# High and low weight parts word by word in one tile, in the feature-major projections of a two-layer decoder trunk

## The chip, the cores and the metric

The kernel runs on one core of a Trainium2 chip. The metric is the device time of one execution in microseconds (us); three timed executions of the kernel before the change gave 2126.0, 2127.0 and 2125.79 us, median 2126.0. The engines in the profile are PE (TensorE, matmuls), PEld (TensorE's weight loads, which overlap PE), DVE (VectorE), ACT (ScalarE), POOL (GpSimd) and SP (SyncE, which here issues the DMAs).

## The reference

A decoder trunk of two layers over 256 positions of width 2048, in fp32. Layer A is a gated mixer beside a cross-attention into 256 memory tokens, layer B a latent attention beside the same cross-attention; each ends in an output projection and a gated feed-forward block of width 5632. Nearly all of the time is in its products with weight matrices:

```python
D_MODEL = 2048; SEQ = 256; DEPTH = 2; D_FF = 5632
...
for l in range(DEPTH):
    if l == N_A:
        kv = rmsnorm(x, g_kv) @ w_kv_a
    ...
    h = rmsnorm(x, g_mix[l])
    z = h @ w_in_a[l]            # layer A: 2048 x 3584; layer B: w_in_b, 2048 x 1024
    ...
    mo = memory_attention(q_m, mem, g_mem[l], w_mem_kv[l])
    x = x + jnp.concatenate([main, mo], axis=-1) @ w_out[l]
    x = x + conv_ffn(rmsnorm(x, g_ffn[l]), w_ffn_up[l], conv_w[l], conv_b[l], w_ffn_down[l])
return rmsnorm(x, g_final)
```

## The kernel before

**Two parts for each operand.** To come near fp32 with the faster matmul type fp32r, each activation and each weight is split in a high part (the value rounded to fp32r) and a low part (what the rounding left). `chunk` makes the two parts of a piece of a weight matrix: a DMA of 512 KB brings 128 x 1024 words into a tile `raw`, ACT writes the high part to a tile `whi` (line 117, or 122 where the rows are scaled by a gain), and DVE writes `raw` minus `whi` to a tile `wlo` (line 118 or 123). There are four tiles of each of the three kinds, used in turn. Each of the tiles holds its 1024 words one behind the other.

**Feature-major projections.** `gemm_fm` computes a product with the features on the partitions: the weights are the stationary operand (128 x 128 words for each matmul), the activations the moving one. A moving tile has 512 columns: 256 of the high part and 256 of the low part. For each 128 x 128 block of weights there are two matmuls: the high weights with all 512 columns (line 140), and the low weights with the 256 high columns (line 144). A call has mostly 16 blocks of 128 rows and 4 blocks of 128 columns, so 64 pairs of matmuls into four PSUM banks; the weights come in 8 chunks, each good for 8 pairs. `mm_fm` takes two chunks at a time (four blocks each in rows and columns) and writes the matmuls out in alternating order: high then low for one couple of chunks, low then high for the next, so that the same kind runs across the seam. When a call is through, its four banks are read out (`evict`): `join` adds the two halves of a bank (ACT line 222, DVE line 224), and in the feed-forward block a multiplication on POOL (line 571), the convolution (ACT line 574, DVE lines 575 and 576) and the gate follow.

**Token-major projections.** `gemm_tm` has the roles swapped: the activations are stationary and the weights move, 512 columns at a time (lines 182 to 184). It serves the memory values, one half of layer A's input projection, layer B's values and the last layer's down projection.

**Order.** The order of each engine's instructions is fixed at build time by a scheduler that replays the program against its own model of the chip; each engine takes its instructions in that order. Tiles come from pools: a tile that is used again waits until all readers of its former content are through. All weight DMAs are issued from SP's queue, each when a `raw` tile is free.

The other callers of `chunk` keep the tiles' layout as it was: `gemm_tm`, the small rotary key projection (`twice`) and layer B's queries (`heads`).

Of the kernel before, what the change touches and what calls it, by code (L numbers as in the profile page):

```python
# [8 lines left out]
F32 = mybir.dt.float32  # L9
F32R = mybir.dt.float32r  # L10
I32 = mybir.dt.int32
BF16 = mybir.dt.bfloat16
AF = mybir.ActivationFunctionType
ALU = mybir.AluOpType
AX = mybir.AxisListType

P = 128
# [13 lines left out]
THETA = 10000.0  # L31
EPS = 1e-6
FF_GROUPS = (4, 4, 3)


def exact_pieces(value, bits, count):
# [33 lines left out]
class Kernel:  # L70
    def __init__(self, ctx, tc, t, out):
        self.tc, self.nc, self.t, self.out = tc, tc.nc, t, out
        self.ctx = ctx
        self.n = 0
        pool = lambda name, bufs=1, **k: ctx.enter_context(tc.tile_pool(name=name, bufs=bufs, **k))
        self.cp = pool("cp")
        self.wp = pool("wp")
        self.ap = pool("ap")
        self.ps = pool("ps", 8, space=bass.MemoryType.PSUM)
# [9 lines left out]
        return pool.tile(shape, dt, tag=tag, name=self.uid(tag), bufs=bufs)  # L89


    def chunk(self, src, nk, ncol, gains=None, twice=False, heads=None):
        nc, n = self.nc, nk * ncol
        raw = self.wp.tile([P, 1024], F32, tag="raw", name=self.uid("raw"), bufs=4)
        hi = self.wp.tile([P, 1024], F32R, tag="whi", name=self.uid("whi"), bufs=4)
        lo = self.wp.tile([P, 1024], F32R, tag="wlo", name=self.uid("wlo"), bufs=4)
        view = lambda x: x[:, :n].rearrange("p (k c) -> p k c", k=nk)
        nc.sync.dma_start(out=view(raw), in_=src)
        if twice:
            both = lambda x: x.rearrange("p (k o c) -> p k o c", o=2, c=ncol)  # L100
            for k in range(nk):
                s = slice(k * ncol, (k + 1) * ncol)
                for o in range(2):
                    h = both(hi)[:, k, o, :]
                    nc.scalar.activation(h, raw[:, s], AF.Copy, scale=gains[k])
                    nc.vector.scalar_tensor_tensor(both(lo)[:, k, o, :], raw[:, s], gains[k], h.bitcast(F32), ALU.mult, ALU.subtract)
            return tuple(x.rearrange("p (k c) -> p k c", k=nk) for x in (hi, lo))
        if heads is not None:

            s = view(raw).rearrange("p k (h c) -> p k h c", h=2)  # L110
            for c0, c1 in ((0, heads), (heads, ncol // 2)):
                o = lambda x: view(x)[:, :, 2 * c0 : 2 * c1].rearrange("p k (h c) -> p k h c", h=2)
                nc.scalar.activation(o(hi), s[:, :, :, c0:c1], AF.Copy)
                nc.vector.tensor_tensor(o(lo), s[:, :, :, c0:c1], o(hi).bitcast(F32), ALU.subtract)
            return view(hi), view(lo)
        if gains is None:
            nc.scalar.activation(hi[:, :n], raw[:, :n], AF.Copy)  # L117
            nc.vector.tensor_tensor(lo[:, :n], raw[:, :n], hi[:, :n].bitcast(F32), ALU.subtract)  # L118
        else:
            for k in range(nk):  # L120
                s = slice(k * ncol, (k + 1) * ncol)
                nc.scalar.activation(hi[:, s], raw[:, s], AF.Copy, scale=gains[k])  # L122
                nc.vector.scalar_tensor_tensor(  # L123
                    lo[:, s], raw[:, s], gains[k], hi[:, s].bitcast(F32), ALU.mult, ALU.subtract
                )
        return view(hi), view(lo)
# [29 lines left out]
            low(jobs)  # L156

    def gemm_fm(self, src, kbs, nblk, rhs, evict, nk=2, gain=None, hooks={}):
        accs = [self.psum() for _ in range(nblk)]
        chunks = list(range(0, len(kbs), nk))  # L160
        for c0 in range(0, len(chunks), 2):
            jobs = []
            for c in chunks[c0 : c0 + 2]:
                g = None if gain is None else [gain(kbs[c + i]) for i in range(nk)]
                hi, lo = self.chunk(src(kbs[c], nk), nk, nblk * P, g)
                for b in range(nblk):
                    cols = slice(b * P, (b + 1) * P)
                    for i in range(nk):
                        kk = c + i
                        jobs.append((accs[b], hi[:, i, cols], lo[:, i, cols], rhs(kbs[kk]), kk == 0, kk == len(kbs) - 1))  # L170
            self.mm_fm(jobs, (c0 // 2) % 2)
            for c in range(c0, min(c0 + 2, len(chunks))):
                for f in hooks.get(c, ()):
                    f()
        for b in range(nblk):
            evict(b, accs[b])
# [154 lines left out]
    def gain(self, name, k):  # L331
        c = self.g[name] + k
        return self.gT[:, c : c + 1]
# [224 lines left out]
    def ffn(self, l, after=None, to_tokens=None, tokens=None):  # L558
# [5 lines left out]
        with self.tc.tile_pool(name=self.uid("ff"), bufs=1) as fp:  # L564
            g0 = 0
            for part, ng in enumerate(FF_GROUPS):
                h = self.ap.tile([P, NB, 512], F32R, tag="big", name=self.uid("h"))
# [11 lines left out]
                for g in range(g0, g0 + ng):  # L579
# [15 lines left out]
                    self.gemm_fm(self.rows(up, FF + g * 512, 512), ks, 4, lambda k: xhl[:, k, :], ev, hooks=turns)  # L595
                last = part == len(FF_GROUPS) - 1
                if last and l == 0:
# [403 lines left out]
```

## Time and profile before

| | |
|---|---|
| median of three executions | 2126.0 us |
| the profiled execution (span) | 2125.1 us |
| PE busy | 2101.5 us |
| DVE busy | 1465.7 us |
| ACT busy | 1148.7 us |
| POOL busy | 392.8 us |
| DMA | 184 GB/s over the span, 59.3% of the 16 engines' time on the weight queue |
| granted TensorE clock | 0.998 |

A row of the view by groups reads: line, engine, operation, output tile, input tiles, partitions x elements of output and inputs, count, then busy time of the group in us and mean ns of one instruction, then the idle time of the engine just before them and what ended most of it. Matmuls overlap, so that the duration of one (390 ns, say) is more than the distance to the next. A row of the timeline merges instructions of one group that follow each other: start, length from the first start to the last end, and count; the distance from one matmul to the next is (length minus the duration of one) over (count minus one).

### The profile page before, as it was taken

What the parts mean: (1) busy time and instruction counts of PE and PEld (TensorE: products, weight loads), DVE (VectorE), ACT (ScalarE), POOL (GpSimd) and SP (SyncE); (2) the same over time, 40 slices, a digit from 0 to 9 for tenths busy, and PEclk for the clock granted to TensorE, in tenths of its full rate; (3) what the DMA queues carried; (4) which work ended last, traced back from release to release, by engine and by line L of the source; (5) the groups of instructions that cost most, each with busy time, mean ns of one, the idle gap of its engine ahead of it and who ended that gap; (6) DMA issues with size and microseconds to landing.
All of it is one profiled execution on the core that took longest, in us unless ns stands there. A gap on an engine that the chain in (4) does not pass through costs nothing.

```text
span 2125.1 us, 31077 instructions
## 1 busy us (share of the span) xinstructions
PE 2101.5 (99%) x11624; PEld 1831.1 (86%) x11624; DVE 1465.7 (69%) x2186; ACT 1148.7 (54%) x1773; POOL 392.8 (18%) x378
## 2 busy tenths in 40 slices
PE   8999999999999999999999999999999999999998
PEld 7888888888888888888888788888888888888886
DVE  6655667777756777567798766677775577745775
ACT  7654654556535555356556554466553555535554
POOL 1000123312101121011254111332120121201210
PEclk9999999999999999999999999999999999999999
DMA  8565555666566665666655533665656666656664
GB/s 272 178 202 178 159 187 189 189 189 191 189 194 187 185 195 188 197 182 188 192 181 165 171 114 110 196 190 170 191 196 195 187 190 190 194 195 188 189 188 149
DMA packets 207548, 392.01 MB, mean 184 GB/s; under 512 B 14302, under 2 KB 22820, under 8 KB 207268
## 3 DMA queue, kind: packets, MB, share of 16 engines
q1 hardware_dynamic: 207252, 389.50, 59.3%
q8 instruction: 91, 1.49, 0.3%
q14 instruction: 61, 0.50, 0.1%
q10 hardware_dynamic: 144, 0.52, 0.1%
HBM read 387.88 MB, written 2.10 MB: 184 GB/s over the span
## 4 chain that ended last, share of the span: by engine, by line
PE 97%; DVE 1%; ACT 1%; DMA 1%; issue 0%; SPq 0%; DVEq 0%; ACTq 0%
PE ps L140 50%; PE ps L144 26%; PE ps L182 6%; PE ps L184 6%; PE ps L183 6%; PE ps L831 1%; DMA raw<-in_w_mem_kv 0%; PE ps L829 0%; PE ps L523 0%; PE ps L488 0%; DVE wlo L118 0%; PE ps L665 0%; PE ps L852 0%; DMA raw<-in_w_in_a 0%; PE ps L393 0%
## 5 line engine op out<-in xcount | busy, mean ns | idle before, releaser
L118 DVE TENSOR_TENSOR wlo<-raw,whi 128x1024 fp32r<-128x1024 f32 x660 | 843.1, 1288 | 490.3 <-ACT whi L117 362.4
L117 ACT ACTIVATE whi<-raw 128x1024 fp32r<-128x1024 f32 x660 | 697.2, 1058 | 702.7 <-PE ps L140 525.4
L140 PE MATMUL ps<-xhl,whi 128*128 128x512 f32 x3280 | 768.9, 390 | 0.0
L140 PEld LDWEIGHTS ps<-xhl,whi 128*128 128x128 f32 x3280 | 608.6, 188 | 121.7
L571 POOL TENSOR_TENSOR a<-js,rbc 128x256 f32<-128x256 f32 x176 | 230.5, 1323 | 1101.7 <-DVE js L224 1005.8
L144 PEld LDWEIGHTS ps<-xhl,wlo 128*128 128x128 f32 x3280 | 408.7, 192 | 9.2 <-DVE wlo L118 0.6
L144 PE MATMUL ps<-xhl,wlo 128*128 128x256 f32 x3280 | 413.4, 283 | 0.4 <-DVE wlo L118 0.4
L140 PE MATMUL ps<-h,whi 128*128 128x512 f32 x704 | 164.8, 390 | 0.0
L574 ACT ACTIVATE c<-a,cT 128x256 f32<-128x256 f32 x176 | 105.2, 598 | 96.9 <-POOL a L571 95.3
L140 PEld LDWEIGHTS ps<-h,whi 128*128 128x128 f32 x704 | 130.6, 188 | 26.0
L183 PE MATMUL ps<-wlo,h 128*128 128x512 f32 x352 | 136.8, 389 | 0.0
L182 PE MATMUL ps<-whi,h 128*128 128x512 f32 x352 | 136.6, 389 | 0.0
L184 PE MATMUL ps<-whi,h 128*128 128x512 f32 x352 | 136.3, 389 | 0.0
L140 PE MATMUL ps<-mainhl,whi 128*128 128x512 f32 x512 | 119.7, 390 | 0.0
L140 PEld LDWEIGHTS ps<-mainhl,whi 128*128 128x128 f32 x512 | 95.1, 188 | 19.1
L123 DVE SCALAR_TENSOR_TENSOR wlo<-raw,gT,whi 128x512 fp32r<-128x512 f32 x112 | 87.9, 829 | 25.2 <-ACT whi L122 23.0
L576 DVE SCALAR_TENSOR_TENSOR c<-a,cT,c 128x254 f32<-128x254 f32 x176 | 101.1, 587 | 0.0
L575 DVE SCALAR_TENSOR_TENSOR c<-a,cT,c 128x255 f32<-128x255 f32 x176 | 91.6, 539 | 11.6 <-ACT c L574 11.4
L122 ACT ACTIVATE whi<-raw,gT 128x512 fp32r<-128x512 f32 x112 | 74.7, 716 | 42.3 <-PE ps L140 20.0
L224 DVE TENSOR_TENSOR js<-ps,cr 128x256 f32<-128x256 f32 x213 | 84.1, 417 | 12.6 <-POOL a L571 12.3
L222 ACT ACTIVATE cr<-ps 128x256 f32<-128x256 f32 x243 | 79.4, 373 | 19.7 <-PE ps L140 16.5
L144 PEld LDWEIGHTS ps<-h,wlo 128*128 128x128 f32 x704 | 87.7, 191 | 2.0
(248 smaller groups left out, 1856.2 us busy)
## 6 DMA issues: line engine op xcount, KB each, us to landing
raw<-in_w_ffn_up SPq DMA_DIRECT2D x352, 512.0 KB, 4.2
raw<-in_w_ffn_down SPq DMA_DIRECT2D x176, 512.0 KB, 4.4
raw<-in_w_out SPq DMA_DIRECT2D x64, 512.0 KB, 4.1
raw<-in_w_in_a SPq DMA_DIRECT2D x56, 512.0 KB, 4.1
raw<-in_w_mem_kv SPq DMA_DIRECT2D x32, 512.0 KB, 4.8
raw<-in_w_in_b SPq DMA_DIRECT2D x16, 512.0 KB, 3.9
raw<-in_w_uq SPq DMA_DIRECT2D x12, 384.0 KB, 3.3
raw<-in_w_kv_a SPq DMA_DIRECT2D x8, 512.0 KB, 4.2
```

What stands on the lines that cost most here:

```text
L117: nc.scalar.activation(hi[:, :n], raw[:, :n], AF.Copy)
L118: nc.vector.tensor_tensor(lo[:, :n], raw[:, :n], hi[:, :n].bitcast(F32), ALU.subtract)
L123: nc.vector.scalar_tensor_tensor(lo[:, s], raw[:, s], gains[k], hi[:, s].bitcast(F32), ALU.mult, ALU.subtract)
L140: mm(acc[:, :], wh, x, start=first, stop=last)
L144: mm(acc[:, S:], wl, x[:, :S], start=False, stop=False)
L182: mm(acc, xh, wh, start=first, stop=False)
L183: mm(acc, xh, wl, start=False, stop=False)
L184: mm(acc, xl, wh, start=False, stop=last)
L571: nc.gpsimd.tensor_tensor(a, self.join(acc), rb, ALU.mult)
L574: nc.scalar.activation(c, a, AF.Identity, scale=w(2), bias=w(3))
L575: nc.vector.scalar_tensor_tensor(c[:, 1:], a[:, : S - 1], w(1), c[:, 1:], ALU.mult, ALU.add)
L576: nc.vector.scalar_tensor_tensor(c[:, 2:], a[:, : S - 2], w(0), c[:, 2:], ALU.mult, ALU.add)
```

## The change

`chunk` gets a new flag `lines`, which `gemm_fm` sets. With it the high and the low part of a chunk stand in one tile `whl` of 2048 + 64 words, word by word: high, low, high, low. ACT writes every second word, DVE reads every second word and writes the ones between, and the weight loads of the two kinds of matmul read 128 words with a step of two. The tile's content begins at `place`, a number of words from 0 to 63 that goes up by one with each call of `gemm_fm` that has four column blocks; over the kernel's 73 such calls it goes through all 64 values. The other callers get their two parts one after the other in the same kind of tile, at its start. There are four tiles `whl` in place of four `whi` and four `wlo`. A scratch area of SBUF for DMA descriptors is made smaller (4096 bytes for each partition), which gives the space for the 64 more words.

```diff
+PLACES = 64
...
+        self.place = 0
...
-        hi = self.wp.tile([P, 1024], F32R, tag="whi", name=self.uid("whi"), bufs=4)
-        lo = self.wp.tile([P, 1024], F32R, tag="wlo", name=self.uid("wlo"), bufs=4)
+        both = self.wp.tile([P, 2048 + PLACES], F32R, tag="whl", name=self.uid("whl"), bufs=4)
         view = lambda x: x[:, :n].rearrange("p (k c) -> p k c", k=nk)
         nc.sync.dma_start(out=view(raw), in_=src)
+        if lines:
+            pairs = both[:, self.place : self.place + 2 * n].rearrange("p (s t) -> p s t", t=2)
+            w, hi, lo = raw[:, :n], pairs[:, :, 0], pairs[:, :, 1]
+            if gains is None:
+                nc.scalar.activation(hi, w, AF.Copy)
+                nc.vector.tensor_tensor(lo, w, hi.bitcast(F32), ALU.subtract)
+            else:
+                for k in range(nk):
+                    s = slice(k * ncol, (k + 1) * ncol)
+                    nc.scalar.activation(hi[:, s], w[:, s], AF.Copy, scale=gains[k])
+                    nc.vector.scalar_tensor_tensor(
+                        lo[:, s], w[:, s], gains[k], hi[:, s].bitcast(F32), ALU.mult, ALU.subtract
+                    )
+            return tuple(x.rearrange("p (k s) -> p k s", k=nk) for x in (hi, lo))
+        hi, lo = both[:, :1024], both[:, 1024:2048]
...
     def gemm_fm(self, src, kbs, nblk, rhs, evict, nk=2, gain=None, hooks={}):
+        if nblk == 4:
+            self.place = (self.place + 1) % PLACES
...
-                hi, lo = self.chunk(src(kbs[c], nk), nk, nblk * P, g)
+                hi, lo = self.chunk(src(kbs[c], nk), nk, nblk * P, g, lines=True)
...
-    nc = bacc.Bacc("TRN2", target_bir_lowering=False, num_devices=1)
+    nc = bacc.Bacc("TRN2", target_bir_lowering=False, num_devices=1, dynamic_dma_scratch_size=4096)
```

The number of instructions of each kind stays the same on all engines, and PE's order changes in a handful of places by a few rows. On ACT and DVE the weight pieces and the evictions trade places. Below stands ACT at the end of one projection and in the next one of the first feed-forward block: `whi` (afterwards `whl`) is the high part of a weight chunk, `cr` and `c` belong to the eviction of a PSUM bank, `gate` and `h` are what the block makes of it. Before:

```order
L117 ACTIVATE whi_6724<-raw_6723 128x1024
L222 ACTIVATE cr_6641<-ps_6434 128x256
L222 ACTIVATE cr_6655<-ps_6435 128x256
L117 ACTIVATE whi_6762<-raw_6761 128x1024
L574 ACTIVATE c_6618<-a_6612,cT 128x256
L574 ACTIVATE c_6632<-a_6626,cT 128x256
L117 ACTIVATE whi_6768<-raw_6767 128x1024
```

and of the change:

```order
L104 ACTIVATE whl_6489<-raw_6488 128x1024
L240 ACTIVATE cr_6409<-ps_6210 128x256
L240 ACTIVATE cr_6423<-ps_6211 128x256
L592 ACTIVATE c_6386<-a_6380,cT 128x256
L592 ACTIVATE c_6400<-a_6394,cT 128x256
L104 ACTIVATE whl_6526<-raw_6525 128x1024
L247 ACTIVATE h_5990<-hv_6390 128x256
```

The high part of the sixth chunk has moved behind two steps of the eviction. DVE in the same block, where `wlo` (afterwards the output `whl`) is the low part of a chunk, `c` the convolution's second and third step, `hv` and `h` the gate's product and its split. Before:

```order
L118 TENSOR_TENSOR wlo_5548<-raw_5546,whi_5547 128x1024
L576 SCALAR_TENSOR_TENSOR c_5418<-a_5412,cT,c_5418 128x254
L589 TENSOR_TENSOR hv_5408<-gate_4993,c_5404 128x256
L118 TENSOR_TENSOR wlo_5554<-raw_5552,whi_5553 128x1024
L575 SCALAR_TENSOR_TENSOR c_5432<-a_5426,cT,c_5432 128x255
```

and of the change:

```order
L594 SCALAR_TENSOR_TENSOR c_5234<-a_5228,cT,c_5234 128x254
L607 TENSOR_TENSOR hv_5224<-gate_4825,c_5220 128x256
L607 TENSOR_TENSOR hv_5238<-gate_4825,c_5234 128x256
L105 TENSOR_TENSOR whl_5359<-raw_5358,whl_5359 128x1024
L248 TENSOR_TENSOR h_3478<-hv_5224,h_3478 128x256
L593 SCALAR_TENSOR_TENSOR c_5248<-a_5242,cT,c_5248 128x255
L105 TENSOR_TENSOR whl_5364<-raw_5363,whl_5364 128x1024
```

The low parts stand two or three rows further back among the eviction's steps.

More of the change, by code (lines that the diff above doesn't have):

```diff
@@ L89, in tmp, with chunk @@
         return pool.tile(shape, dt, tag=tag, name=self.uid(tag), bufs=bufs)
-    def chunk(self, src, nk, ncol, gains=None, twice=False, heads=None):
+    def chunk(self, src, nk, ncol, gains=None, twice=False, heads=None, lines=False):
         nc, n = self.nc, nk * ncol
         raw = self.wp.tile([P, 1024], F32, tag="raw", name=self.uid("raw"), bufs=4)
-        hi = self.wp.tile([P, 1024], F32R, tag="whi", name=self.uid("whi"), bufs=4)
-        lo = self.wp.tile([P, 1024], F32R, tag="wlo", name=self.uid("wlo"), bufs=4)
+        both = self.wp.tile([P, 2048 + PLACES], F32R, tag="whl", name=self.uid("whl"), bufs=4)
         view = lambda x: x[:, :n].rearrange("p (k c) -> p k c", k=nk)
         nc.sync.dma_start(out=view(raw), in_=src)
+        if lines:
[13 more added lines that the diff above has]
+        hi, lo = both[:, :1024], both[:, 1024:2048]
         if twice:
-            both = lambda x: x.rearrange("p (k o c) -> p k o c", o=2, c=ncol)
+            four = lambda x: x.rearrange("p (k o c) -> p k o c", o=2, c=ncol)
             for k in range(nk):
@@ L103, in chunk @@
                 for o in range(2):
-                    h = both(hi)[:, k, o, :]
+                    h = four(hi)[:, k, o, :]
                     nc.scalar.activation(h, raw[:, s], AF.Copy, scale=gains[k])
-                    nc.vector.scalar_tensor_tensor(both(lo)[:, k, o, :], raw[:, s], gains[k], h.bitcast(F32), ALU.mult, ALU.subtract)
+                    nc.vector.scalar_tensor_tensor(four(lo)[:, k, o, :], raw[:, s], gains[k], h.bitcast(F32), ALU.mult, ALU.subtract)
             return tuple(x.rearrange("p (k c) -> p k c", k=nk) for x in (hi, lo))
```

## The prediction

> **What bounds the kernel now.** I read the busy times first, then the chain of waits, then who waited for whom.
>
> ```profile
> PE 2101.5 (99%) x11624; PEld 1831.1 (86%) x11624; DVE 1465.7 (69%) x2186; ACT 1148.7 (54%) x1773; POOL 392.8 (18%) x378
> PE 97%; DVE 1%; ACT 1%; DMA 1%; issue 0%; SPq 0%; DVEq 0%; ACTq 0%
> PE ps L140 <- DVE qhl L235: 3.7, 1, 3.7
> PE ps L144 <- DVE wlo L118: 0.4, 1, 0.4
> ```
>
> TensorE is busy for 99% of the span, the chain is TensorE's for 97%, and its waits for others are a few single ones. So a gain can only come from matmuls that follow each other faster, and a loss from slower matmuls, from weight loads that no longer fit beside them, or from weight parts that come too late.
>
> How fast matmuls follow each other is read from the timeline of one couple of chunks in the feed-forward block, beside the groups by line:
>
> ```profile
> 396.27 4.00 PE L144 MATMUL ps<-xhl,wlo 128*128 128x256 f32 x32
> 400.10 7.44 PE L140 MATMUL ps<-xhl,whi 128*128 128x512 f32 x32
> L140 PE MATMUL ps<-xhl,whi 128*128 128x512 f32 x3280 | 768.9, 390 | 0.0
> L144 PE MATMUL ps<-xhl,wlo 128*128 128x256 f32 x3280 | 413.4, 283 | 0.4 <-DVE wlo L118 0.4
> L140 PEld LDWEIGHTS ps<-xhl,whi 128*128 128x128 f32 x3280 | 608.6, 188 | 121.7
> L144 PEld LDWEIGHTS ps<-xhl,wlo 128*128 128x128 f32 x3280 | 408.7, 192 | 9.2 <-DVE wlo L118 0.6
> ```
>
> Low matmuls: (4.00 - 0.283) / 31 = 0.120 us from one to the next. High ones: (7.44 - 0.390) / 31 = 0.227 us. A pair takes 0.347 us. The last column of the two load rows is what matters: beside high matmuls the loads stand idle for 121.7 us, beside low ones for 9.2 us in all. In the low runs the next load goes on nearly without a pause, so there the load has little room.
>
> How many pairs does the change touch? The groups give the counts:
>
> ```profile
> L140 PE MATMUL ps<-h,whi 128*128 128x512 f32 x704 | 164.8, 390 | 0.0
> L140 PE MATMUL ps<-mainhl,whi 128*128 128x512 f32 x512 | 119.7, 390 | 0.0
> L140 PE MATMUL ps<-memhl,whi 128*128 128x512 f32 x128 | 32.9, 410 | 3.5 <-DVE memhl L440 2.5 <-ACT whi L122 1.0
> L140 PE MATMUL ps<-chl,whi 128*128 128x512 f32 x48 | 13.5, 400 | 0.0
> ```
>
> 3280 + 704 + 512 + 128 + 48 = 4672, less the 16 of the rotary key projection, which keeps its layout: 4656 pairs in 582 chunks. One ns more or less on each pair is 4.7 us; 4656 x 0.347 us = 1616 us, three quarters of the span, is exposed to the change.
>
> **The change part by part.**
>
> *Weight loads with a step of two words.* The trace has no load with a step, so I bound it. A load alone, without a longer matmul over it, shows where plain fp32 matmuls of 128 columns follow each other, and a faster kind of load shows in the transposes:
>
> ```profile
> 1246.26 0.30 PEld L863 LDWEIGHTS ps<-pT,scratch 128*128 128x128 f32 x2
> L512 PEld LDWEIGHTS ps<-ident,mp 128*128 128x128 f32 x32 | 3.7, 140 | 0.8 <-PE ps L512 0.7
> L488 PEld LDWEIGHTS ps<-kT,qm 128*128 128x128 f32 x32 | 5.9, 190 | 0.9
> L488 PE MATMUL ps<-kT,qm 128*128 128x256 f32 x32 | 7.6, 379 | 0.0
> L937 PE MATMUL ps<-ident,xT 128*128 128x128 f32 x32 | 3.8, 272 | 0.0
> ```
>
> Two loads in 0.30 us, the last of them 0.19 us long, lie about 0.11 us apart: a load holds its path for some 110 ns, and in the low runs it has 120. Its room is about 10 ns. The transposes load just as many words (128x128 f32) in 140 ns where the others need 190, so fetching the same 512 bytes can take 50 ns less; I estimate from these rows that a plain load leaves about half of the read rate unused. With a step of two it reads a stretch twice as long at the same number of words, which would use up that rate but not exceed it. Upper bound: the load takes twice its 110 ns, the low matmuls then follow each other at some 220 ns, and the high ones stay at 227: 4656 x 0.10 = +466 us. Lower bound: the matmuls gain what fp32r costs over plain fp32, 390 against 379 ns for a matmul that streams as long, and 283 against 272 ns for the shorter one: 11 + 11 ns on each pair, 4656 x 0.022 = -102 us. I take 0, since the load needs 110 of 120 ns and the transposes' row says that the fetch has a rate in hand.
>
> The Trainium skill, in "SBUF — State Buffer", section "Specifications (TRN2)", says that SBUF is read in lines of 16 bytes and that full rate needs at least two hits on each line; a step of two words has exactly two, so by it the load stays as it is, and the sum too. No run here shows it.
>
> *The writes on ACT and DVE.* The number of words is the same, but ACT writes and DVE reads and writes with a step.
>
> ```profile
> L117 ACT ACTIVATE whi<-raw 128x1024 fp32r<-128x1024 f32 x660 | 697.2, 1058 | 702.7 <-PE ps L140 525.4 <-PE ps L184 140.4 <-ACT h L229 8.4
> L118 DVE TENSOR_TENSOR wlo<-raw,whi 128x1024 fp32r<-128x1024 f32 x94 | 120.4, 1292 | 59.6 <-ACT whi L117 41.2 <-PE ps L144 15.8 <-issue 2.6
> 370.00:630.00 260.00, 260.00 (x1494) 230.07 (x1493) 186.03 (x261) 141.02 (x198) 50.14 (x40) 1.00 0.62 189
> 1080.00:1200.00 120.00, 116.34 (x635) 101.39 (x634) 102.20 (x172) 69.18 (x139) 43.27 (x46) 0.97 0.55 174
> ```
>
> The two window rows give the busy time of PE, PEld, DVE, ACT and POOL. In the feed-forward stretch from 370 to 630 us DVE is busy for 186.0 of 260 us, 120.4 of them on the low parts (94 at 1292 ns, the second row, which is of this stretch). Nothing of their price shows until DVE is full: (260 - 186) / 120.4 = 0.61, so up to a factor of 1.6 TensorE covers it there. ACT has more room: 141 of 260. Lower bound 0. Upper bound: twice the time, 186 + 120 = 306 against 260 us, 18% on the 1616 us of pairs, +290 us. I take 0: 1292 ns for 1024 words is already slower than ACT's 1058, so the memory that takes ACT's words is not what holds DVE.
>
> *Four tiles in place of eight.* High and low part now come free together, so ACT's next high part waits for both kinds of matmul. What stands there now:
>
> ```profile
> 450.22 1.06 ACT L117 ACTIVATE whi<-raw 128x1024 fp32r<-128x1024 f32 x1 [0.74 <-PE ps L140]
> 451.83 4.00 PE L144 MATMUL ps<-xhl,wlo 128*128 128x256 f32 x32
> 453.04 2.36 DVE L118 TENSOR_TENSOR wlo<-raw,whi 128x1024 fp32r<-128x1024 f32 x2 [2.31 <-PE ps L144]
> 455.67 6.54 PE L140 MATMUL ps<-xhl,whi 128*128 128x512 f32 x28
> ```
>
> ACT wrote the high part at 450.22, as soon as the high matmuls of the old one were through. Now it waits for that chunk's low matmuls, the first eight of the run from 451.83: until 451.83 + 8 x 0.12 = 452.8. DVE can then begin at 453.9 in place of 453.04, 0.9 us later. The chunk's first use is after the other couple's 16 high matmuls, at 455.67 + 16 x 0.227 = 459.3, and its low part is needed later still. So 0.9 us disappears in more than 4 us of room. Behind ACT's wait stand the evictions in its queue, and the `raw` tile is free 0.9 us later, hence the next DMA; both have the same room. It can show where DVE is tight: from 1080 to 1200 us (last row of the windows above) it is busy for 102 of 120 us. There and in the eleven other calls of the two mixers and output projections I allow up to 0.9 us a call, bounds 0 and some 15 x 0.9 = 13 us, and take 4, a third, since most of these calls look like the stretch above.
>
> *The order on ACT and DVE, and the scratch area.* The weight pieces stand two or three rows further back among the evictions. Two convolution steps are about 1.1 us; that lies within the same room. All DMAs of weights are SP's, and their order is the same: 0.
>
> *Sum.* 2125.1 (the profiled execution) + 0 + 0 + 4 = 2129, and with the 0.9 us by which the median lies above this execution, **2130 us**.
>
> **The rivals.**
>
> *The load no longer fits (slower).* Place: the low runs. It decides from the point where a load takes over about 117 ns, 7% more than now. What speaks for it: the loads' idle time there is 9.2 us, no reserve at all. Against it: the transposes' 140 ns. Price: at a quarter more, 138 ns, the low matmuls follow each other at about 140 and not 120 ns, 4656 x 0.02 = +93 us, 2219 us. If the load took a share of the moving operand's reading, and twice as much as now, each of the two matmuls of a pair would pay its 11 ns a second time: +102 us, 2228 us. At twice the load, 2592 us.
>
> *DVE becomes the bound (slower).* From a factor of 1.6 on. Halfway between that and twice the time, at 1.8, DVE would need 186 + 96 = 282 of 260 us, 8.6% of 1616 us: +139 us, 2265 us. For it: DVE has two operands with the step, and 72% is its share already. Against it: nothing in the trace shows that a step of 8 bytes costs anything.
>
> The Trainium skill, in "Vector Engine (DVE) Microarchitecture Reference", section "5.2 Measured stream behaviour on trn2 (trn3 not measured)", speaks against the change: a port keeps its rate only over runs of two or more adjacent words, and an output that hops at each word took 1.71 ns for a column against 1.054. As an estimate from that page, L118 would be 1.6 times as long, just where DVE is full; a step of two words is not among its cases, and no run here shows it.
>
> *The matmuls get faster.* If fp32r's extra 11 ns come from weight words and moving words that meet in the same part of the memory, then another step and another place change it: for half of the places this would be -51 us, 2079 us; for all of them -102 us, 2028 us. For it: both kinds of matmul pay the same 11 ns although one is half as long, as if it came with the weights and not with the columns. Against it: the means of 390 ns are the same for moving tiles that lie in different places (the rows of `xhl`, `h` and `mainhl`).
>
> *It does nothing.* The four tiles cost nothing either: 2126 us. This is the forecast without its last term.
>
> **How the numbers follow.** I give the forecast, with 2124 to 2140 as its own range, 0.43; the load 0.23 (of this 0.07 for over 2300); DVE 0.12; the faster matmuls 0.15; other things, an order on ACT and DVE that happens to be better or worse, 0.07. What can be told from no change is 0.2%, 4.3 us. Of the forecast's 0.43, 0.23 lies within that and 0.17 above, 0.03 below. Faster: 0.15 + 0.03 + 0.02 = 0.20. Same: 0.23 + 0.01 = 0.24. Slower: 0.17 + 0.23 + 0.12 + 0.04 = 0.56. Range: 2095 leaves out two thirds of the faster case (0.10), 2300 the heavy end of the load and of DVE (0.07 + 0.03).
>
> **What would show it.** The profile of the changed kernel: the distance of low matmuls within a run (120 ns: the load fits; 140 or 220: it doesn't) and of high ones (227 ns; 216: the faster case; 238: a shared read); the loads' mean of 192 and 188 ns, and their idle time in low runs; the mean of the high part on ACT (1058 ns) and of the low part on DVE (1288 ns); DVE's idle time before the low part, which should now be ACT's doing alone; and TensorE's waits, which should stay below 20 us in all. If the distances differ from projection to projection, the place matters. The forecast is wrong if TensorE's distance in the runs moves by more than 1 ns, or if its waits for DVE grow by tens of us.

## The result and the profile after

The changed kernel takes 2154.9 us (median of four executions, 2154.5 to 2156.1): 1.0132 times the kernel before, with a 95% interval of 1.0118 to 1.0147. The profiled execution has a span of 2154.4 us, 29.3 us more than the 2125.1 before, at a granted clock of 0.996.

The busy times of the changed kernel:

```profile
PE 2127.1 (99%) x11624; PEld 1869.5 (87%) x11624; DVE 1470.4 (68%) x2186; ACT 1190.4 (55%) x1773; POOL 367.9 (17%) x378
```

The counts of instructions in this row are those of the kernel before. PE's busy time grew from 2101.5 to 2127.1 us, by 25.6; its idle time, span less busy, from 23.6 to 27.3 us, by 3.7. So nearly nine tenths of the loss lie in matmuls that follow each other more slowly, and the rest in waits. The groups that answer to those before (L156 was L140, L160 was L144; L104 and L105 write the two parts):

```profile
L156 PE MATMUL ps<-xhl,whl 128*128 128x512 f32 x3280 | 785.1, 395 | 0.0
L160 PE MATMUL ps<-xhl,whl 128*128 128x256 f32 x3280 | 415.3, 284 | 3.3 <-DVE whl L110 2.8
L156 PEld LDWEIGHTS ps<-xhl,whl 128*128 128x128 f32 x3280 | 632.8, 196 | 113.0
L160 PEld LDWEIGHTS ps<-xhl,whl 128*128 128x128 f32 x3280 | 411.9, 197 | 11.9 <-DVE whl L110 3.0
L104 ACT ACTIVATE whl<-raw 128x1024 fp32r<-128x1024 f32 x542 | 613.0, 1148 | 552.0 <-PE ps L160 258.9
L105 DVE TENSOR_TENSOR whl<-raw,whl 128x1024 fp32r<-128x1024 f32 x542 | 688.7, 1284 | 418.0 <-ACT whl L104 416.9
```

The busy time of a group of overlapping matmuls is a count times their distance, so its growth tells the distance's. The high matmuls on `xhl` have 785.1 - 768.9 = 16.2 us more, 4.9 ns each; the low ones 1.9 us, 0.6 ns each. These 18.1 us over 3280 pairs make 25.7 us over all 4656, which is PE's whole growth. The timeline shows it without a mean, in the projection that stands near the one quoted before:

```profile
402.07 4.04 PE L160 MATMUL ps<-xhl,whl 128*128 128x256 f32 x32
405.95 7.56 PE L156 MATMUL ps<-xhl,whl 128*128 128x512 f32 x32
```

High: (7.56 - 0.395) / 31 = 0.231 us in place of 0.227. Low: (4.04 - 0.284) / 31 = 0.121 in place of 0.120. Neither is the price of a load that no longer fits: the loads' idle time beside high matmuls is still 113 us, and the low runs, where the load has least room, lose almost nothing. The other projections have other distances, from 0.230 to 0.234 us for high matmuls and 0.118 to 0.122 us for low ones.

The waits of TensorE for low parts, in the view by releaser (us in total, times, longest), and where the two long ones stand in the timeline:

```profile
PE ps L160 <- DVE whl L110: 2.8, 1, 2.8
PE ps L160 <- DVE whl L105: 1.7, 2, 1.3
...
1076.01 1.25 PE L160 MATMUL ps<-h,whl 128*128 128x256 f32 x8 [1.26 <-DVE whl L105]
1181.90 1.89 PE L160 MATMUL ps<-xhl,whl 128*128 128x256 f32 x8 [2.83 <-DVE whl L110]
```

Before, the only wait for a low part was 0.4 us. These rows add 4.1 us, and small shifts of other waits leave the 3.7 us of idle time.

### The profile page after: what moved, and what is told of

Same layout as the page of the kernel before. It is cut to its first block, busy times and chain, and to the rows that moved or that the text cites. A ratio compares the mean times of both kernels' runs of the same rounds, so it can differ in the third digit from the quotient of the medians.

```text
span 2154.4 us, 31000 instructions
## 1 busy us (share of the span) xinstructions
PE 2127.1 (99%) x11624; PEld 1869.5 (87%) x11624; DVE 1470.4 (68%) x2186; ACT 1190.4 (55%) x1773; POOL 367.9 (17%) x378
## 4 chain that ended last, share of the span: by engine, by line
PE 96%; DVE 1%; ACT 1%; DMA 1%; issue 0%; SPq 0%; DVEq 0%; ACTq 0%
PE ps L156 50%; PE ps L160 26%; PE ps L200 6%; PE ps L202 6%; PE ps L201 6%; PE ps L849 1%; PE ps L847 0%; PE ps L541 0%; DMA mtok<-in_mem 0%; PE ps L506 0%; ACT whl L109 0%; DMA raw<-in_w_mem_kv 0%; DVE whl L105 0%; ACT junk L423 0%; PE ps L683 0%
## 5 line engine op out<-in xcount | busy, mean ns | idle before, releaser
L105 DVE TENSOR_TENSOR whl<-raw,whl 128x1024 fp32r<-128x1024 f32 x542 | 688.7, 1284 | 418.0 <-ACT whl L104 416.9
L104 ACT ACTIVATE whl<-raw 128x1024 fp32r<-128x1024 f32 x542 | 613.0, 1148 | 552.0 <-PE ps L160 258.9
L156 PE MATMUL ps<-xhl,whl 128*128 128x512 f32 x3280 | 785.1, 395 | 0.0
L156 PEld LDWEIGHTS ps<-xhl,whl 128*128 128x128 f32 x3280 | 632.8, 196 | 113.0
L160 PEld LDWEIGHTS ps<-xhl,whl 128*128 128x128 f32 x3280 | 411.9, 197 | 11.9 <-DVE whl L110 3.0
L160 PE MATMUL ps<-xhl,whl 128*128 128x256 f32 x3280 | 415.3, 284 | 3.3 <-DVE whl L110 2.8
L134 DVE TENSOR_TENSOR whl<-raw,whl 128x1024 fp32r<-128x1024 f32 x118 | 145.7, 1239 | 120.3 <-ACT whl L133 120.0
L133 ACT ACTIVATE whl<-raw 128x1024 fp32r<-128x1024 f32 x118 | 124.3, 1058 | 146.7 <-PE ps L202 114.7
L156 PE MATMUL ps<-h,whl 128*128 128x512 f32 x704 | 167.9, 394 | 0.0
L156 PEld LDWEIGHTS ps<-h,whl 128*128 128x128 f32 x704 | 135.9, 196 | 23.7
L201 PE MATMUL ps<-whl,h 128*128 128x512 f32 x352 | 136.8, 389 | 0.0
L202 PE MATMUL ps<-whl,h 128*128 128x512 f32 x352 | 136.3, 389 | 0.0
L200 PE MATMUL ps<-whl,h 128*128 128x512 f32 x352 | 136.1, 389 | 0.0
L156 PE MATMUL ps<-mainhl,whl 128*128 128x512 f32 x512 | 122.4, 396 | 0.0
L156 PEld LDWEIGHTS ps<-mainhl,whl 128*128 128x128 f32 x512 | 99.0, 196 | 17.8
L160 PEld LDWEIGHTS ps<-h,whl 128*128 128x128 f32 x704 | 88.5, 197 | 3.3 <-DVE whl L105 1.5
L160 PE MATMUL ps<-h,whl 128*128 128x256 f32 x704 | 88.9, 283 | 1.3 <-DVE whl L105 1.3
```

The costliest lines, as they stand in the source:

```text
L104: nc.scalar.activation(hi, w, AF.Copy)
L105: nc.vector.tensor_tensor(lo, w, hi.bitcast(F32), ALU.subtract)
L156: mm(acc[:, :], wh, x, start=first, stop=last)
L160: mm(acc[:, S:], wl, x[:, :S], start=False, stop=False)
L200: mm(acc, xh, wh, start=first, stop=False)
L201: mm(acc, xh, wl, start=False, stop=False)
```

## The experiments

All are compared with the kernel before, executed in turn with them (2127.4 us in the first set, 2127.1 in the second, 2128.5 for the two kernels that were executed once, 2126.2 in the last).

### One joint tile without step and places

```diff
-                hi, lo = self.chunk(src(kbs[c], nk), nk, nblk * P, g, lines=True)
+                hi, lo = self.chunk(src(kbs[c], nk), nk, nblk * P, g)
```

> High and low part one behind the other in the one tile again, no step, no place; the single tile, its four buffers and the smaller scratch area stay. If the step of the weight loads (with or without the place) is what costs: high matmuls 226.7 ns apart as before, low ones 120, time 2126 to 2130 us. If the joint release of the two parts, the order on ACT and DVE or the scratch area costs: about 2150 us, with more waits of TensorE.

Measured: 2131.5 us, ratio 1.0020 (1.0010 to 1.0029). Its groups and its wait:

```profile
L156 PE MATMUL ps<-xhl,whl 128*128 128x512 f32 x3280 | 769.6, 391 | 0.0
L160 PE MATMUL ps<-xhl,whl 128*128 128x256 f32 x3280 | 414.7, 284 | 3.5 <-DVE whl L139 3.0
PE ps L160 <- DVE whl L139: 3.0, 1, 3.0
PE ps L160 <- DVE whl L134: 1.8, 2, 1.3
```

The matmuls are back at the distances of before, the two waits stay. So the joint tile, with the order that follows from it and the smaller scratch area, costs 4 us, and the step and the place cost the rest: 2154.9 less 2131.5, some 23 us.

### Step of two at one place

```diff
-        self.place = 0
+        self.place = 19
...
-        if nblk == 4:
-            self.place = (self.place + 1) % PLACES
```

One kernel with place 19 for all projections, and one with 0, which keeps the first of these lines as it was.

> The step of two stays, the place is 0 in all projections. If the step costs and the place only shapes it: the projections of the changed kernel with place 0 had 234.2 ns between high matmuls and 119.8 between low ones, 7.4 ns a pair more than before, so 4656 x 7.4 = +34 us, 2160 us. If it is starts off a 256-byte boundary that cost: 226.7 and 120 ns, about 2127 us. If the place is without effect: as the changed kernel, 2155 us.

> The step of two, place 19 in all projections, the one with the smallest sum in the changed kernel: 230.2 and 118.8 ns, 2.4 ns a pair more than before. If the place shapes the cost: 2126 + 11 = 2137 us. If what differed between projections was not the place: as the changed kernel, 2155 us. If only starts off the boundary cost: at least 2155 us.

Measured: place 0 2162.1 us, ratio 1.0167 (1.0152 to 1.0182); place 19 2142.1 us, 1.0071 (1.0056 to 1.0086). The high group at place 0, and two of its runs that follow each other:

```profile
L156 PE MATMUL ps<-xhl,whl 128*128 128x512 f32 x3280 | 792.6, 397 | 0.0
405.35 7.62 PE L156 MATMUL ps<-xhl,whl 128*128 128x512 f32 x32
416.64 7.70 PE L156 MATMUL ps<-xhl,whl 128*128 128x512 f32 x32
```

792.6 - 769.6 = 23.0 us over 3280, 7.0 ns for each high matmul. With the same step everywhere, the place alone moves the time by 20 us; the sweep of the changed kernel lies between the two. The times are 2 and 5 us above what the distances of the changed kernel's projections at these places had given (2160 and 2137 us), and those sums left out the 4 us of the joint tile. So at these two places its distances carry over to a kernel that keeps the place.

The two runs show that step and place are not all that counts. Their matmuls stand 0.233 and 0.236 us apart ((7.62 - 0.397) / 31 and (7.70 - 0.397) / 31), and in the feed-forward block the runs go on alternating like this. By the order of the program both runs take all four tiles in the same turn, with the same step and the same place. What differs between them stays open.

### Places without a step

```diff
-            w, hi, lo = raw[:, :n], pairs[:, :, 0], pairs[:, :, 1]
+            w, hi, lo = raw[:, :n], both[:, self.place : self.place + n], both[:, 1024 + self.place : 1024 + self.place + n]
```

> No step, but each projection's two parts start at its place, 0 to 63 words from the tile's two halves. If the step costs: 2126 to 2131 us, high matmuls within 1 ns of 226.7. If starts off the boundary cost: about 2150 us, the more the further from a multiple of four words. If a place can also help, some projections are under 226.7 ns or under 120 ns.

Measured: 2145.1 us, ratio 1.0087 (1.0070 to 1.0104). The theory that the step alone is to blame has fallen: 13.6 us of the loss appear with every part contiguous, from the place.

```profile
L155 PE MATMUL ps<-xhl,whl 128*128 128x512 f32 x3280 | 783.9, 395 | 0.0
L159 PE MATMUL ps<-xhl,whl 128*128 128x256 f32 x3280 | 410.2, 282 | 3.4 <-DVE whl L109 2.9
398.81 3.93 PE L159 MATMUL ps<-xhl,whl 128*128 128x256 f32 x32
402.58 7.63 PE L155 MATMUL ps<-xhl,whl 128*128 128x512 f32 x32
488.41 3.79 PE L159 MATMUL ps<-xhl,whl 128*128 128x256 f32 x32
```

The high matmuls are slower ((7.63 - 0.395) / 31 = 0.233 us here), but the low ones are faster: 410.2 us against 414.7 without places. At a few places they follow each other at 0.113 to 0.114 us, as in the last row, which is of place 16: (3.79 - 0.282) / 31 = 0.113.

### Which of the two steps costs

The high part with a step of two from the tile's start and the low part contiguous behind it, in a tile of 3072 words; and the reverse.

```diff
-        both = self.wp.tile([P, 2048 + PLACES], F32R, tag="whl", name=self.uid("whl"), bufs=4)
+        both = self.wp.tile([P, 3072], F32R, tag="whl", name=self.uid("whl"), bufs=4)
...
-            pairs = both[:, self.place : self.place + 2 * n].rearrange("p (s t) -> p s t", t=2)
-            w, hi, lo = raw[:, :n], pairs[:, :, 0], pairs[:, :, 1]
+            pairs = both[:, : 2 * n].rearrange("p (s t) -> p s t", t=2)
+            w, hi, lo = raw[:, :n], pairs[:, :, 0], both[:, 2048 : 2048 + n]
```

The longer tile gets its space from a still smaller scratch area (256 bytes).

> Only the high parts lie with a step of two words, the low parts one after the other behind them, both at place 0. Theory A (the step costs where a high matmul runs beside the load of the next high part, because that load then touches twice as many memory lines and takes turns from the moving operand): high 234 ns apart as with both stepped at place 0, low 120.0 ns, so about 2131.5 + 4656 x 7.5 ns = 2166 us less what ends of runs give back, 2158 to 2167. Rival B (the cost comes from where the operand begins against the moving operand, not from the step): high 226.7, low between 113 and 120, time 2100 to 2132.

> Only the low parts lie with a step of two words, at place 0; the high parts lie contiguously. Theory A: high stays 226.7 ns; low 119 to 122 ns, as with both stepped; time 2128 to 2140 us. Rival B (the place alone decides): low as with the contiguous low part at place 0, 120.0 ns, time 2131. A low matmul near 127 ns (2164 us) would say that each of the two widths pays the same for the step.

Measured: the high part's step 2153.3 us, ratio 1.0129 (1.0112 to 1.0146), 5 us below the 2158 to 2167 that theory A had named; the low part's step 2131.9 us, 1.0023 (1.0014 to 1.0033), the same as no step at all. A run of each kind from the timeline, first with the high part's step:

```profile
403.87 7.61 PE L156 MATMUL ps<-xhl,whl 128*128 128x512 f32 x32
411.32 3.99 PE L160 MATMUL ps<-xhl,whl 128*128 128x256 f32 x32
```

then with the low part's:

```profile
402.28 7.44 PE L156 MATMUL ps<-xhl,whl 128*128 128x512 f32 x32
409.56 4.00 PE L160 MATMUL ps<-xhl,whl 128*128 128x256 f32 x32
```

(7.61 - 0.394) / 31 = 0.233 us for the high matmuls with their own step, 0.227 with the low part's. The low matmuls stay at 0.120 in both. So the price of the step lies on the high matmuls, which have the most room for their loads. The two steps apart cost 21.8 and 0.4 us against 2131.5, but both together at place 0 cost 30.6 (2162.1). In a run of high matmuls only high weights are loaded, and these stand at the same words of the tile in both kernels; yet the full runs have 0.233 us here and every second one 0.236 there. The kernels also differ in the tile's length, and no run separates that from the low part's layout. So the cause of these 8 us stays open.

### The load by itself

The kernel with the high part's step, with narrow matmuls. The first high matmul of a projection keeps its 512 columns; the rest of the product is left out.

```diff
-                mm(acc[:, :], wh, x, start=first, stop=last)
+                w = 512 if first else 16
+                mm(acc[:, :w], wh, x[:, :w], start=first, stop=last)
...
-                mm(acc[:, S:], wl, x[:, :S], start=False, stop=False)
+                mm(acc[:, S : S + 16], wl, x[:, :16], start=False, stop=False)
```

> High parts with a step of two, low parts contiguous; every high matmul but a projection's first, and every low one, takes only 16 columns of its moving operand (the rest of the product is left out), so that in a run the distance of two matmuls is the weight load alone. If a load with a step of two takes as long as one without (the load was not what made the high matmuls slower, the sharing of the memory with the moving operand was): both about the same, near 60 to 110 ns. If it reads twice the lines at the same pace: the high runs' distance is up to twice that of the low runs, and above 120 ns it would have shown in the low matmuls of the stepped low part, so 100 to 120 against 55 to 110. The total time says nothing here, since ScalarE and VectorE become the bound.

Executed once, it took 2556.0 us at a mean granted clock of 0.598, so only its stretches at the full clock can be compared with the other kernels. L157 are now the loads with a step of two, L161 those without. From the timeline, with the row that follows the low run:

```profile
71.32 1.93 PE L161 MATMUL ps<-memhl,whl 128*128 128x16 f32 x16
73.11 1.09 PE L410 MATMUL ps<-ident,xtok 128*128 128x128 f32 x8
...
198.40 2.38 PE L157 MATMUL ps<-xhl,whl 128*128 128x16 f32 x19
...
342.67 6.97 PE L157 MATMUL ps<-mainhl,whl 128*128 128x16 f32 x32
349.50 6.97 PE L161 MATMUL ps<-mainhl,whl 128*128 128x16 f32 x32
```

and the windows around them (busy time of PE, PEld, DVE, ACT, POOL, then granted clock, DMA share, GB/s):

```profile
71.40:73.10 1.70, 1.70 (x17) 1.70 (x16) 0.66 (x1) 0.66 (x2) 0.00 (x0) 1.00 0.06 22
198.40:200.40 2.00, 2.00 (x19) 2.00 (x19) 2.00 (x6) 0.88 (x1) 0.00 (x0) 1.00 0.89 249
320.00:330.00 10.00, 10.00 (x48) 10.00 (x48) 2.97 (x3) 2.26 (x2) 0.00 (x0) 0.50 0.56 171
```

Without step: (73.11 - 71.32) / 16 = 0.112 us for a load, and the last narrow matmul takes 1.93 - 15 x 0.112 = 0.25 us. With a step of two: (2.38 - 0.25) / 18 = 0.118 us. So at the full clock the step makes the load about 6 ns longer (by the starts in the trace, the other stretches at the full clock have the same two distances), and it still fits into the 120 ns of a low matmul, just. At a granted clock of 0.50 the two runs are equally long, 6.97 us for 32: there the load takes about 0.213 us with or without a step. So the step's 6 ns show only at the full clock. That they belong to the fetch, and that at half the clock the array's own work is the slower of the two, would fit this; no run shows the two apart.

### A step of three

Every third word of a tile of 3072, from its start:

```diff
-            pairs = both[:, self.place : self.place + 2 * n].rearrange("p (s t) -> p s t", t=2)
+            pairs = both[:, : 3 * n].rearrange("p (s t) -> p s t", t=3)
```

> High and low parts lie with a step of three words (the third word unused), place 0: each load then spans 1536 bytes of a partition in place of 1024 (step of two) or 512. If the cost grows with the lines touched (theory A): high about 238 to 241 ns and the time 2175 to 2200 us. If the load no longer fits beside the low matmul of 120 ns: low well above 125 ns, time above 2200. If the step matters only by its phase (rival B): high anywhere from 227 to 236 ns, low 113 to 122, time 2125 to 2165.

Measured: 2417.4 us, ratio 1.1369 (1.1352 to 1.1386).

```profile
413.92 5.67 PE L160 MATMUL ps<-xhl,whl 128*128 128x256 f32 x32
L156 PE MATMUL ps<-xhl,whl 128*128 128x512 f32 x3280 | 800.0, 399 | 0.1
L160 PE MATMUL ps<-xhl,whl 128*128 128x256 f32 x3280 | 585.0, 336 | 2.3 <-DVE whl L110 1.5
L156 PEld LDWEIGHTS ps<-xhl,whl 128*128 128x128 f32 x3280 | 767.1, 253 | 1.2 <-DVE js L240 0.3
L104 ACT ACTIVATE whl<-raw 128x1024 fp32r<-128x1024 f32 x542 | 856.3, 1605 | 534.0 <-PE ps L160 225.0
L105 DVE TENSOR_TENSOR whl<-raw,whl 128x1024 fp32r<-128x1024 f32 x542 | 882.0, 1644 | 469.5 <-ACT whl L104 469.1
```

Here the load no longer fits: low matmuls (5.67 - 0.336) / 31 = 0.172 us apart, 1.4 times the 0.120 of before, and the loads' idle time beside high matmuls is gone (1.2 us). This is the picture of the rival that the forecast weighed, at a step of three and not at two. ACT at 1605 and DVE at 1644 ns pay here too, and TensorE still stands idle before these low matmuls for only 2.3 us.

### The place of the low part alone

No step, the high part at the start of the tile in every projection; the low part 16 words later than in the joint tile, or in a sweep, whose edit this is:

```diff
-            w, hi, lo = raw[:, :n], pairs[:, :, 0], pairs[:, :, 1]
+            w, hi, lo = raw[:, :n], both[:, :n], both[:, 1024 + self.place : 1024 + self.place + n]
```

> No step: high parts contiguous at place 0, low parts contiguous behind them, begun 16 words (64 bytes) later than in the joint tile without places. If the distance of the matmuls depends on where the weights begin (as the sweep of places without a step suggests, where place 16 had its low matmuls 113.3 ns apart): high 226.7 ns, low 113.3 ns, 4656 x 6.7 ns = 31 us less than the joint tile without places, about 2100 us (2098 to 2106). Rival: the sweep's low distances came from the high part's place or from the change of place between projections, and the time stays at 2131 us with low 120.0 ns.

> No step: high parts contiguous at the start of the joint tile in every projection, low parts contiguous behind them, begun at a place that sweeps all multiples of 4 bytes. If the low matmul's distance is set by where its own weights begin: high 226.7 ns throughout, place 16 again 117.8 ns as in the run with that place alone, other places between 113 and 122 ns; the mean of the sweep gives 2118 to 2128 us. If it also hangs on the high part's place (which moved along in the earlier sweep without a step): the low distances differ from that sweep's place by place, above all at 16, where it had 113.3 ns. If the high matmuls lose 4 to 7 ns again although their weights do not move, the change of place between projections is itself the cost: 2140 us or more.

Measured: at 16 words 2121.1 us, ratio 0.9975 (0.9965 to 0.9984); the sweep, executed once, 2125.3 us beside 2128.5 for the kernel before. At 16 words the low matmuls stand (3.93 - 0.281) / 31 = 0.118 us apart, not 0.113:

```profile
406.26 3.93 PE L159 MATMUL ps<-xhl,whl 128*128 128x256 f32 x32
```

So the price given for that run, 2100 us, was too hopeful: in the first sweep the high part had moved to 16 as well, and the low distance hangs on that too. The second sweep bears this out: its low matmuls at place 16 (the second row below) stand 0.118 us apart again. The high matmuls keep their speed there (their group has 769.4 us), and the low distance goes with the low part's place; the last three rows are places 19, 21 and 22:

```profile
L155 PE MATMUL ps<-xhl,whl 128*128 128x512 f32 x3280 | 769.4, 391 | 0.0
485.06 3.93 PE L159 MATMUL ps<-xhl,whl 128*128 128x256 f32 x32
551.40 3.81 PE L159 MATMUL ps<-h,whl 128*128 128x256 f32 x32
595.38 4.00 PE L159 MATMUL ps<-h,whl 128*128 128x256 f32 x32
617.63 3.81 PE L159 MATMUL ps<-h,whl 128*128 128x256 f32 x32
```

(3.81 - 0.281) / 31 = 0.114 us at 19 and 22, 0.120 at 21. Both places had 0.114 in the first sweep too.

### The kernel before with its low part moved

```diff
-        lo = self.wp.tile([P, 1024], F32R, tag="wlo", name=self.uid("wlo"), bufs=4)
+        lo = self.wp.tile([P, 1088], F32R, tag="wlo", name=self.uid("wlo"), bufs=4)[:, at : at + 1024]
...
-                hi, lo = self.chunk(src(kbs[c], nk), nk, nblk * P, g)
+                hi, lo = self.chunk(src(kbs[c], nk), nk, nblk * P, g, at=19)
...
-    nc = bacc.Bacc("TRN2", target_bir_lowering=False, num_devices=1)
+    nc = bacc.Bacc("TRN2", target_bir_lowering=False, num_devices=1, dynamic_dma_scratch_size=4096)
```

and the same with 22.

> The kernel before, its high and low parts in tiles of their own, with the feature-major low parts begun 19 words (76 bytes) into a low tile that is 64 words longer. If the low matmul's distance follows the place of its own weights, as in the sweep of the low place alone (113.7 ns at 19, high 227.4): about 4656 x 6.2 ns = 29 us less than before, so 2096 to 2100 us at its own run of before's 2127. If it hangs on more than the place in the tile (the tile's own address, the kernel's other tiles): anything between 113 and 122 ns, 2096 to 2136 us.

> As the kernel before with its feature-major low parts at 19 words, but at 22 words, where the sweep of the low place alone also had 113.8 ns: again 2096 to 2100 us, if the place in the tile decides; should only one of 19 and 22 be fast, the tile's own address or the state in which a run of low matmuls begins counts as well.

Measured: 2100.5 us with 19, ratio 0.9874 (0.9858 to 0.9891); 2100.7 us with 22, 0.9877 (0.9862 to 0.9892). Both beat the kernel before by 1.2%, and the changed one by 2.5%. With 19:

```profile
PE 2075.5 (99%) x11624; PEld 1804.7 (86%) x11624; DVE 1466.2 (70%) x2186; ACT 1147.3 (55%) x1773; POOL 393.1 (19%) x378
L144 PE MATMUL ps<-xhl,wlo 128*128 128x256 f32 x3280 | 394.8, 277 | 0.5 <-DVE wlo L118 0.4
398.02 7.44 PE L140 MATMUL ps<-xhl,whi 128*128 128x512 f32 x32
405.30 3.81 PE L144 MATMUL ps<-xhl,wlo 128*128 128x256 f32 x32
```

394.8 us against 413.4, so 5.7 ns less for each low matmul, times 4656 26 us: that is the gain, and PE's busy time fell by just as much (2101.5 to 2075.5). The high matmuls keep their distance, and the order of PE, DVE, ACT and POOL is that of the kernel before, instruction by instruction. The longer low tile and the smaller scratch area have not been run with the low part at the tile's start, so what they do by themselves is not shown; the two places were named beforehand from the sweep.

## Why the prediction was right in sign and wrong in mechanism

The forecast was 2130 us with its own range of 2124 to 2140; 2154.9 lies above that, inside the wide range of 2095 to 2300. That it still lies there is luck: the upper part of the range stood for a load that no longer fits and for a full DVE, and neither came. Of the 29 us only the 4 of the four tiles were forecast. The text named its own test, a distance in the runs that moves by more than 1 ns, and the high matmuls moved by 5.

- *Weight loads with a step of two, taken as 0.* **This is the step that failed.** It asked only whether the load still fits beside the matmul, and it does: 0.118 of 0.120 us, where the estimate had 110 of 120 ns and a fetch with "a rate in hand". The rate was not quite in hand (6 ns more), and, what counts, the high matmuls, whose loads need only about half of their 0.227 us, got slower. The term was 25.6 us of TensorE's time in place of 0, from the step and the place together. The place had no term of its own in the sum, only a rival, and costs 13.6 us without any step. The bounds, -102 and +466, held it.
- *The rule of the Trainium skill beside it* ("SBUF — State Buffer", "Specifications (TRN2)": two hits on each 16-byte line keep the full rate) agrees in tendency: at a step of three the low matmuls, and so the loads that hold them up, stand 0.172 us apart, against 0.112 for a load without a step. At a step of two, which has its two hits, the load went from 0.112 to 0.118 us and the high matmuls from 0.227 to 0.233, so there the measurement decides against "the load stays as it is". The same row of the Trainium skill adds that each cross to a new line pays a penalty, which the prediction left out.
- *The writes on ACT and DVE, taken as 0.* Right for the time. ACT's high part took 1148 ns in place of 1058, hidden behind TensorE as said; DVE's low part did not change (1288 to 1284 ns), and its idle time is now ACT's doing alone, as foretold. The estimate from the Trainium skill, "Vector Engine (DVE) Microarchitecture Reference", "5.2 Measured stream behaviour on trn2 (trn3 not measured)", 1.6 times as long, did not come true at a step of two; at three it was 1644 / 1284 = 1.28.
- *Four tiles in place of eight, taken as 4 us.* The size held: 3.7 us of idle time here, 4 us in the kernel with the joint tile alone. Its form was other than described, so the size is luck in part. It is not up to 0.9 us at each of many calls but nearly all of it in two waits of the low matmuls: 2.8 us in layer B's first projections, at 1182 us, near the end of the stretch that was named as tight, and 1.3 us at 1076 us.
- *The rivals.* "The load no longer fits" is what a step of three does. At a step of two the load passed the 117 ns from which this rival was to decide, if only just, and the low matmuls stayed at 0.120 us. Its second form, a share of the moving operand's reading, is nearest to what is seen, but its price of 11 ns on both kinds of matmul (+102 us) was wrong in size and place: about 5 ns, on the high ones. "DVE becomes the bound" didn't come. "The matmuls get faster" had the right lead, that the place of the weights moves the distance, and the wrong kernel: in the changed one no place comes out ahead of before (by the starts of the matmuls in the trace, the two distances of a pair make at best 0.349 us, at place 19, and 0.347 before), since the high matmuls lose more than the low ones gain; without a step and with the high part left where it was, the low matmuls gain 6 ns. What was held against it (the same means for three moving tiles) spoke of moving tiles only; the weights' place had never been varied.

What is shown: the step of the high part alone costs the high matmuls 6 ns at the tile's start (6 to 9 with both parts stepped) and the low part's step alone nothing; the sweep of places costs the high matmuls (783.9 - 769.6) / 3280 = 4.4 ns on the mean without any step; the place of the low part alone gives up to 6 ns back. Step and place don't add: at place 0 the step costs 31 us (2162.1 less 2131.5), the sweep of places 14 us, both together 23 us. With the same place and step, the runs still alternate between 0.233 and 0.236 us.

What stays open: why a load of 0.118 us delays a matmul of 0.227 us and not one of 0.120 us; by which rule the places are good or bad, and what makes every second run slower at place 0; and why place 16 gives 0.113 us when the high part has moved along and 0.118 when it hasn't. That load and moving operand meet in the memory would fit slower and faster places, but no run shows the meeting itself; and the load's own 6 ns need none, since they are there with hardly any columns to stream.

## What to carry to other kernels

That a weight load is hidden beside its matmul doesn't say that its layout is free: read the distance of the matmuls themselves, not only whether the load fits. Here it paid to keep stationary operands contiguous and to try where they begin: a sweep that gives each projection another place shows all places in one trace, and here a shift of 76 bytes of the low weights alone was worth 1.2% of the kernel. Vary one operand's place at a time: place 16 of the low part lost most of its gain when the high part stayed behind. Look at single runs and not only at means, and measure a good place again in the kernel that is to keep it.

## What the runs showed of the hardware that was not expected

- The distance of matmuls with the same shapes and the same granted clock depends on where the stationary operand begins, in words: 0.114 us at 19 and 22 and 0.120 at 21 for 256 columns, and 0.227 us at the tile's start against 0.233 in the row of the sweep for 512. With one step and one place it still alternates between 0.233 and 0.236 us from run to run.
- A step of two words in ACT's output costs 8.5% (1058 to 1148 ns), one of three words 52% (1605 ns). On DVE two cost nothing and three 28%.
- Weight loads back to back with hardly any columns to stream brought the granted clock down to 0.50 (the window from 320 to 330 us), with TensorE and its loads busy without a pause; the kernels with full matmuls had 0.996 to 0.999.
